# Down-projection of a transformer block: the subtraction for a chunk's own columns moved behind its block sums on VectorE

## The chip, the cores and the metric

The kernel runs on one core of a Trainium2 chip. The metric is the time of one execution on the device in microseconds (us), as the median of several executions. The profile is of one further execution, taken by the hardware profiler. Engines: TensorE (PE in the profile, PEld for its weight loads), VectorE (DVE), ScalarE (ACT), GpSimd (POOL) and SyncE (SP, here a DMA queue).

## The reference

One residual block on 512 tokens of width 1024: two attention branches with gates, then a gated convolutional feed-forward part, whose end is what this case is about.

```python
def conv_glu(x, w_up, conv_w, conv_b, w_down):
    hid = x @ w_up
    hid = lax.conv_general_dilated(hid, conv_w[:, None, :], window_strides=(1,),
        padding=((CONV_WIDTH - 1, 0),), dimension_numbers=('NWC', 'WIO', 'NWC'),
        feature_group_count=2 * D_FF) + conv_b
    gate, up = hid[..., :D_FF], hid[..., D_FF:]
    return (jax.nn.silu(gate) * up) @ w_down
...
    x = x + (sigmoid(g_A) * y_A + sigmoid(g_B) * y_B) @ w_out
    x = x + conv_glu(rms_norm(x, norm2_g), w_ffn_up, ffn_conv_w, ffn_conv_b, w_ffn_down)
```

The down-projection multiplies 512 x 2816 by 2816 x 1024, all in float32.

## The kernel before, in words

**Numbers in two parts.** A float32 matrix product is made of three matmuls of a reduced format (float32r): each operand is split into a high part (a cast, on ScalarE) and a low part (the original minus the cast, on VectorE), and high by high, high by low and low by high are added up in PSUM. For weights, the function `split_gen` issues the cast (line 148) and the subtraction (line 150).

**Chunks and loads.** The weights come in chunks of 1 MB or, for the down-projection, 0.5 MB, in a fixed order that `CHUNKS` lists. While TensorE multiplies with one chunk, `run_chunk` steps the generator that splits the next one, and when a chunk's split ends, the load of a later chunk goes to SyncE's queue (line 104). In the down-projection the raw weights lie in three thirds of a ring, each 1024 columns wide, and a chunk's load goes to the third of the chunk three before it. It waits until that chunk's readers are done.

**Fast matrix product.** The down-projection runs in two passes (`s` = 0, 1), each for 512 of the 1024 output columns, and each in 11 chunks of 256 of the 2816 inner columns. A chunk is a 2 x 2 product of blocks and is made in Winograd's form with 7 products (line 855 gives their order: 1, 2, 3, 6, 5, 7, 4) instead of 8. Each product has two tiles of 128 tokens and three matmuls of 256 columns each (lines 875 to 877), so a chunk has 42 matmuls. Of the weight operands, three of the seven are blocks of the raw chunk itself (its own columns, 768 wide; products 1, 2 and 3 use them), and four are sums and differences of blocks (1024 wide; products 6, 5, 7 and 4). `down_sums` makes these four on VectorE with three instructions (lines 118, 119 and 120), in a scratch area of 1024 columns that all chunks share. So a chunk is split in two pieces, with one cast and one subtraction each: first the own columns, then the sums.

**Where the split weights lie.** Up to the fifth chunk of the second pass the high and the low parts each have two buffers (`whi`, `wlo`), so that a cast waits for the end of the chunk before last. From the sixth chunk of the second pass they lie in a pool of eight (`hl`), whose buffers the operands `a` of the first eight chunks leave behind as they are used up.

**The order of instructions.** It is not that of the code: a planner simulates the engines and sorts the instructions of each engine by its own estimate of when they can run. `behind(ins, others)` (line 537) sets an order by hand, without a wait on the chip: the planner puts `ins` after `others` on their engine. `late["halves"]` is the last subtraction of a down-projection chunk, and each subtraction is put behind the one before it (line 153); some of the adds that put results together are put behind it too (lines 903, 905, 924, 927, 941). `late["casts"]` does the same for the casts.

**Putting together.** `fin0` and `rest0` combine the seven products of the first pass with adds (line 881 is the helper `add`), and `rest0` spreads its eight adds over the second pass's chunks, one for each, the last two at the very end. Each pass has seven product banks out of eight in PSUM, so that the second pass's products take over banks that the first pass's adds and copies free. In the second pass the last two chunks are multiplied together (`ends`, lines 991 to 1005): products 1, 6 and 2 of the one, then of the other, then product 5 of both, 7 of both, 4 of both, and at last 3. `fin1` adds them to the residual and stores: line 958 subtracts product 4, line 963 adds product 3 in two halves, and each result goes to a store.

Of the kernel before, what the change touches and what calls it, by code (L numbers as in the profile page):

```python
# [11 lines left out]
ALU = mybir.AluOpType  # L12
# [52 lines left out]
def block_kernel(ctx: ExitStack, tc: tile.TileContext, x, xt, params, g2, rbx, wts, wdn, out):  # L65
    nc = tc.nc
    V, A, G, PE, SP = nc.vector, nc.scalar, nc.gpsimd, nc.tensor, nc.sync
# [26 lines left out]
    raws, splits, late, ring = {}, {}, {}, []  # L94
# [18 lines left out]
    def down_sums(raw):  # L113

        b = raw.rearrange("p (b c) -> p b c", c=256)
        ts = ring[1][:, 1024:2048]
        t = ts.rearrange("p (b c) -> p b c", c=256)
        V.tensor_tensor(t[:, 0:2], b[:, 0:4:2], b[:, 0:2][:, ::-1], op=ALU.subtract)
        V.tensor_tensor(t[:, 2], b[:, 2], t[:, 0], op=ALU.subtract)
        V.tensor_tensor(t[:, 3], t[:, 2], b[:, 3], op=ALU.subtract)  # L120
        return ts

    def split_gen(i, pieces):
# [11 lines left out]
        if i >= FIRST_DN:  # L135

            if i < FIRST_DN + NP + 5:
                hi, lo = hi[:, 0:1792], lo[:, 0:1792]
            else:
                hl = late["pool"].tile([P, 3584], F32R, tag="ap", name=f"hl_{key}", bufs=8)  # L140
                hi, lo = hl[:, 0:1792], hl[:, 1792:3584]
            cuts, kn = [(0, raw[:, 256:1024]), (768, down_sums(raw))], 7
# [394 lines left out]
    def behind(ins, others):  # L537

        for o in others:
            tc.add_manual_dep(ins.ins, o.ins.name, mybir.DependencyInfo(  # L540
                mybir.DependencyClass.NoSync, mybir.DependencyReason.DATA), reason="table order")
        return ins
# [104 lines left out]
    for s in range(len(steps)):  # L647
# [6 lines left out]
        br, h, t, e = pend.pop(0)  # L654
# [171 lines left out]
    halves = []  # L826
# [51 lines left out]
        return prev  # L878

    def add(o, a, b, op=ALU.add, after=()):  # L880
        behind(V.tensor_tensor(o, a, b, op=op), after)

    def blk(x, r, c):

        return x[:, 2 * r:2 * r + 2, 256 * c:256 * (c + 1)]

    v3 = lambda ap: ap.rearrange("p (t c) -> p t c", t=2)
# [8 lines left out]
    def fin0(p):  # L896
        ps = banks[0][p]
        c = tmp["c"]
        if p == 1:
            tmp["u"] = fp.tile([P, S], F32, tag="cg", name="u_0", bufs=1)  # L900
            A.copy(tmp["u"], ps)
        elif p == 2:
            add(blk(c, 0, 0), v3(ps), v3(tmp["u"]), after=late["halves"])
        elif p == 6:
            add(tmp["u"], ps, tmp["u"], after=late["halves"])
        elif p == 5:
            tmp["v"] = fp.tile([P, 768], F32, tag="st", name="v_0", bufs=1)[:, 0:S]
            add(tmp["v"], ps, tmp["u"])
        elif p == 7:
            behind(A.copy(blk(c, 1, 1), v3(ps)), late["casts"])  # L910
        elif p == 4:
            behind(A.mul(blk(c, 1, 0), v3(ps), -1.0), late["casts"])
        else:
            behind(A.copy(blk(c, 0, 1), v3(ps)), late["casts"])
# [16 lines left out]
    def fin1(p):  # L931
        ps = banks[1][p]
        x = tmp["x"]

        def put(r, c):
            for t in range(2 * r, 2 * r + 2):
                SP.dma_start(out[0, t * P:(t + 1) * P, 512 + 256 * c:768 + 256 * c], x[:, t, 256 * c:256 * (c + 1)])
        if p == 1:
            tmp["u"] = fp.tile([P, S], F32, tag="cg", name="u_1", bufs=1)
            behind(A.copy(tmp["u"], ps), late["casts"])  # L940
            add(blk(x, 0, 0), v3(ps), blk(x, 0, 0), after=late["halves"])
        elif p == 6:
            add(tmp["u"], ps, tmp["u"])
        elif p == 2:
            add(blk(x, 0, 0), v3(ps), blk(x, 0, 0))
            put(0, 0)
        elif p == 5:
            tmp["v"] = fp.tile([P, 768], F32, tag="st", name="v_1", bufs=1)[:, 0:S]
            add(tmp["v"], ps, tmp["u"])
            add(blk(x, 1, 1), blk(x, 1, 1), v3(tmp["v"]))  # L950
            add(blk(x, 0, 1), blk(x, 0, 1), v3(tmp["v"]))
            add(blk(x, 1, 0), blk(x, 1, 0), v3(tmp["u"]))
        elif p == 7:
            add(blk(x, 1, 1), v3(ps), blk(x, 1, 1))
            put(1, 1)
            add(blk(x, 1, 0), v3(ps), blk(x, 1, 0))
        elif p == 4:
            add(blk(x, 1, 0), blk(x, 1, 0), v3(ps), op=ALU.subtract)
            put(1, 0)
        else:  # L960
            for t in range(2):
                o = x[:, t, 256:512]
                add(o, ps[:, 256 * t:256 * (t + 1)], o)
                (SP, A)[t].dma_start(out[0, t * P:(t + 1) * P, 768:1024], o)

    rest = iter(())
# [26 lines left out]
    for ps in ((1, 6, 2), (5,), (7,), (4,)):  # L993
        for i, (hi, lo) in ends:
            for p in ps:
                prev = product(1, p, i, hi, lo, prev=prev)
                if i == NP - 1:
                    fin1(p)
                    if p < 3:
                        for _ in range(2):  # L1000
                            next(rest, None)
    for t in range(2):
        for i, (hi, lo) in ends:
            prev = product(1, 3, i, hi, lo, (t,), prev)
    fin1(3)


# [39 lines left out]
```

## Time and profile before

| what | us |
|---|---|
| median of 3 runs | 749.35 (749.09 to 749.73) |
| the profiled execution, its own time | 749.92 |
| its span, first to last instruction | 748.2 |
| down-projection, first to last matmul | 626.0 to 744.1 |
| last matmul's end to the span's end | 4.05 |

How to read the profile: times are us from the start of the span, unless marked ns. A row of a timeline gives start, duration, engine, line of the kernel, operation, what it writes and reads, its shape, and how many instructions are merged in it; in brackets stands the idle time of the engine before it, and whose work ended it. A row of stretches gives the limits of the stretch, its length, the busy time of an engine with the number of instructions, the granted clock of TensorE as a share of full speed, the share of time in which the DMA engines were busy, and GB/s. The chain of waits follows the work that ended last backwards; a row gives start, length and what ran. Ends of matmuls are modelled: a busy TensorE need not be at its peak.

### The profile page before, as it was taken

What the parts mean: (1) busy time and instruction counts of PE and PEld (TensorE: products, weight loads), DVE (VectorE), ACT (ScalarE), POOL (GpSimd) and SP (SyncE); (2) the same over time, 40 slices, a digit from 0 to 9 for tenths busy, and PEclk for the clock granted to TensorE, in tenths of its full rate; (3) what the DMA queues carried; (4) which work ended last, traced back from release to release, by engine and by line L of the source; (5) the groups of instructions that cost most, each with busy time, mean ns of one, the idle gap of its engine ahead of it and who ended that gap; (6) DMA issues with size and microseconds to landing.
All of it is one profiled execution on the core that took longest, in us unless ns stands there. A gap on an engine that the chain in (4) does not pass through costs nothing.

```text
span 748.2 us, 10982 instructions
## 1 busy us (share of the span) xinstructions
PE 737.1 (99%) x4301; PEld 648.2 (87%) x4301; DVE 536.8 (72%) x984; ACT 377.3 (50%) x674; POOL 41.8 (6%) x73
## 2 busy tenths in 40 slices
PE   8999999999999999999999999999999999999996
PEld 7999998888988888888899888888888889999995
DVE  6588876776978886573476777676668767877776
ACT  6675565557856775432254544534444443434331
POOL 2701100001011011000000000000000000000000
PEclk9999999999999999999999999999999999999998
DMA  8632232122221131225341232233133211333442
GB/s 283 262 123 85 83 115 72 62 92 73 65 105 57 57 108 62 92 106 224 113 169 64 107 112 87 84 112 113 57 113 113 71 71 57 113 112 116 140 141 85
DMA packets 19205, 79.98 MB, mean 107 GB/s; under 512 B 2128, under 2 KB 4304, under 8 KB 13008
## 3 DMA queue, kind: packets, MB, share of 16 engines
q1 hardware_dynamic: 18864, 79.04, 30.2%
q8 instruction: 34, 0.56, 0.3%
q10 hardware_dynamic: 288, 0.23, 0.1%
q14 instruction: 19, 0.16, 0.1%
HBM read 75.07 MB, written 4.19 MB: 106 GB/s over the span
## 4 chain that ended last, share of the span: by engine, by line
PE 90%; DVE 5%; ACT 2%; issue 2%; DMA 1%; SPq 0%; DVEq 0%
PE pg L176 5%; PE pu L176 5%; PE pu L175 5%; PE pg L175 5%; PE pu L177 5%; PE pg L177 5%; PE P L876 3%; PE P L877 3%; PE P L875 3%; PE gA L175 2%; PE wo L176 2%; PE wo L177 2%; PE wo L175 2%; PE gA L177 2%; PE qkB L175 2%; PE gB L175 2%
## 5 line engine op out<-in xcount | busy, mean ns | idle before, releaser
L150 DVE TENSOR_TENSOR wlo_up<-raw_up,whi_up 128x1024 fp32r<-128x1024 f32 (+1 forms) x50 | 52.4, 1094 | 51.0 <-ACT whi_up L148 51.0
L176 PE MATMUL pu<-htl,whi_up 128*128 128x512 f32 (+1 forms) x192 | 72.1, 375 | 0.0
L176 PE MATMUL pg<-htl,whi_up 128*128 128x512 f32 (+1 forms) x192 | 72.0, 375 | 0.0
L175 PE MATMUL pu<-hth,whi_up 128*128 128x512 f32 (+1 forms) x192 | 71.7, 374 | 0.0
L175 PE MATMUL pg<-hth,whi_up 128*128 128x512 f32 (+1 forms) x192 | 71.7, 374 | 0.0
L177 PE MATMUL pg<-hth,wlo_up 128*128 128x512 f32 (+1 forms) x192 | 71.1, 370 | 0.0
L177 PE MATMUL pu<-hth,wlo_up 128*128 128x512 f32 (+1 forms) x192 | 71.0, 370 | 0.0
L148 ACT CAST whi_up<-raw_up 128x1024 fp32r<-128x1024 f32 (+1 forms) x50 | 44.6, 945 | 30.9 <-PE pu L176 27.2
L876 PE MATMUL P<-wlo_dn,a 128*128 128x256 f32 x224 | 59.2, 281 | 0.0
L877 PE MATMUL P<-whi_dn,a 128*128 128x256 f32 x224 | 59.0, 280 | 0.0
L875 PE MATMUL P<-whi_dn,a 128*128 128x256 f32 x224 | 50.3, 282 | 0.5 <-ACT whi_dn L148 0.5
L148 ACT CAST whi_dn<-raw_dn 128x768 fp32r<-128x768 f32 (+1 forms) x32 | 29.1, 942 | 42.8 <-DVE raw_dn L120 38.2
L150 DVE TENSOR_TENSOR wlo_dn<-raw_dn,whi_dn 128x768 fp32r<-128x768 f32 (+1 forms) x32 | 34.2, 1089 | 20.6 <-ACT whi_dn L148 20.5
L876 PEld LDWEIGHTS P<-wlo_dn,a 128*128 128x128 f32 x224 | 42.3, 189 | 0.3
L877 PEld LDWEIGHTS P<-whi_dn,a 128*128 128x128 f32 x224 | 42.3, 189 | 0.0
L175 PEld LDWEIGHTS pu<-hth,whi_up 128*128 128x128 f32 x192 | 36.0, 188 | 7.1
L175 PEld LDWEIGHTS pg<-hth,whi_up 128*128 128x128 f32 x192 | 36.0, 188 | 7.0
L177 PEld LDWEIGHTS pu<-hth,wlo_up 128*128 128x128 f32 x192 | 36.0, 188 | 6.7
L177 PEld LDWEIGHTS pg<-hth,wlo_up 128*128 128x128 f32 x192 | 36.0, 188 | 6.7
L176 PEld LDWEIGHTS pu<-htl,whi_up 128*128 128x128 f32 x192 | 36.1, 188 | 6.0
L176 PEld LDWEIGHTS pg<-htl,whi_up 128*128 128x128 f32 x192 | 36.1, 188 | 5.9
L875 PEld LDWEIGHTS P<-whi_dn,a 128*128 128x128 f32 x224 | 36.6, 188 | 1.2 <-ACT whi_dn L148 1.2
(260 smaller groups left out, 2065.7 us busy)
## 6 DMA issues: line engine op xcount, KB each, us to landing
raw_up<-in_wts SPq DMA_DIRECT2D x22, 1024.0 KB, 4.7
raw_dn<-in_wdn SPq DMA_DIRECT2D x22, 512.0 KB, 3.2
raw_gA<-in_wts SPq DMA_DIRECT2D x4, 1024.0 KB, 4.7
raw_qkB<-in_wts SPq DMA_DIRECT2D x4, 1024.0 KB, 4.7
raw_gB<-in_wts SPq DMA_DIRECT2D x4, 1024.0 KB, 4.7
raw_wo<-in_wts SPq DMA_DIRECT2D x4, 1024.0 KB, 4.7
xs<-in_xt SPq DMA_DIRECT2D x8, 256.0 KB, 5.0
xtok<-in_x SPq DMA_DIRECT2D x4, 512.0 KB, 7.7
```

What stands on the lines that cost most here:

```text
L148: cast = A.copy(hi[:, sl], src)
L150: ins = E.tensor_tensor(lo[:, sl], src, hi[:, sl].bitcast(F32), op=ALU.subtract)
L175: PE.matmul(ps, sh, mh, start=first, stop=False)
L176: PE.matmul(ps, sh, ml, start=False, stop=False)
L177: PE.matmul(ps, sl, mh, start=False, stop=last)
L875: behind(PE.matmul(dst, sh, mh, start=first and t == 0, stop=False, skip_group_check=True), prev)
L876: PE.matmul(dst, sh, ml, start=False, stop=False, skip_group_check=True)
L877: prev = (PE.matmul(dst, sl, mh, start=False, stop=last, skip_group_check=True),)
```

## The change

In `down_sums`, the last of the three instructions is added to `late["halves"]`. The first subtraction of the same chunk's split, that of the own columns, is issued right after, and so is put behind it: on VectorE the order within a chunk becomes sums, own columns' subtraction, sums' subtraction. Before, nothing set the order between the sums and the own columns' subtraction. From the own columns' subtraction on, `late["halves"]` is what it was.

The second part is at the end of the second pass: the subtraction of product 4 (line 958) is kept in `late["p4"]`, and the two adds of product 3 (line 963), the product issued last, are put behind it on VectorE.

```diff
@@ -117,7 +117,9 @@
         t = ts.rearrange("p (b c) -> p b c", c=256)
         V.tensor_tensor(t[:, 0:2], b[:, 0:4:2], b[:, 0:2][:, ::-1], op=ALU.subtract)
         V.tensor_tensor(t[:, 2], b[:, 2], t[:, 0], op=ALU.subtract)
-        V.tensor_tensor(t[:, 3], t[:, 2], b[:, 3], op=ALU.subtract)
+        ins = V.tensor_tensor(t[:, 3], t[:, 2], b[:, 3], op=ALU.subtract)
+
+        late["halves"] = late.get("halves", ()) + (ins,)
         return ts
@@ -878,7 +880,7 @@
     def add(o, a, b, op=ALU.add, after=()):
-        behind(V.tensor_tensor(o, a, b, op=op), after)
+        return behind(V.tensor_tensor(o, a, b, op=op), after)
@@ -955,12 +957,12 @@
         elif p == 4:
-            add(blk(x, 1, 0), blk(x, 1, 0), v3(ps), op=ALU.subtract)
+            late["p4"] = (add(blk(x, 1, 0), blk(x, 1, 0), v3(ps), op=ALU.subtract),)
             put(1, 0)
         else:
             for t in range(2):
                 o = x[:, t, 256:512]
-                add(o, ps[:, 256 * t:256 * (t + 1)], o)
+                add(o, ps[:, 256 * t:256 * (t + 1)], o, after=late["p4"])
                 (SP, A)[t].dma_start(out[0, t * P:(t + 1) * P, 768:1024], o)
```

## The prediction

> **What bounds the kernel now.** I read the page first, then TensorE's matmuls of the down-projection by stretches of time, then the rounds of VectorE and ScalarE that feed them. The page says that TensorE is the bound:
>
> ```profile
> span 748.2 us, 10982 instructions
> PE 737.1 (99%) x4301; PEld 648.2 (87%) x4301; DVE 536.8 (72%) x984; ACT 377.3 (50%) x674; POOL 41.8 (6%) x73
> ```
>
> That is an average. The change touches only the down-projection, 22 chunks of 42 matmuls (7 products, 2 token tiles, 3 matmuls each). The next rows are busy time and, in brackets, the number of matmuls on the product banks P in each stretch; behind it the granted clock. The two rows below them are from the chain of waits, where TensorE is the chain.
>
> ```profile
> 642.00:696.00 54.00, 54.00 (x463) 1.00 0.39 127
> 696.00:728.20 32.20, 32.05 (x254) 1.00 0.40 132
> 728.20:735.90 7.70, 4.55 (x31) 1.00 0.00 0
> 735.90:739.30 3.40, 3.40 (x18) 0.50 0.41 154
> 739.30:744.20 4.90, 4.85 (x40) 1.00 0.32 107
> 696.00:744.20 48.20, 44.85 (x338) 0.96 0.33 110
> ```
> ```profile
> 649.00 0.82 PE P L875 x7
> 653.95 0.82 PE P L875 x7
> ```
>
> Two rows of the chain, one chunk apart, give the undisturbed pitch: 4.95 us for 42 matmuls, 117.9 ns each. At that pitch the 338 matmuls from 696.0 to 744.2 need 39.85 us; they took 48.2. So **8.35 us are lost in the last eight chunks**, though the busy column calls TensorE busy for 44.85 of them (a matmul's span there is 0.28 us, so busy time hides a gap of 0.1 us). In the same way 254 x 0.1179 = 29.95 of 32.2 (2.25 lost), 3.65 of 7.7 (4.05 lost), 2.1 of 3.4 (1.3 lost, at half the clock), 4.7 of 4.9. (A matmul over an edge counts in both stretches, so these parts come out a little under the whole.)
>
> Who makes TensorE late? One round of VectorE, and ScalarE's rows beside it:
>
> ```profile
> 703.26 1.23 DVE L150 TENSOR_TENSOR wlo_dn<-raw_dn,whi_dn 128x1024 fp32r<-128x1024 f32 x1 [1.12 <-ACT whi_dn L148]
> 704.41 0.68 DVE L881 TENSOR_TENSOR c<-c,v 128x512 f32<-128x512 f32 x1
> 705.01 0.95 DVE L150 TENSOR_TENSOR hl_dn<-raw_dn,hl_dn 128x768 fp32r<-128x768 f32 x1
> 705.88 0.68 DVE L118 TENSOR_TENSOR raw_dn<-raw_dn 128x512 f32<-128x512 f32 x1
> 706.60 0.42 DVE L119 TENSOR_TENSOR raw_dn<-raw_dn,raw_dn 128x256 f32<-128x256 f32 x1
> 707.05 0.43 DVE L120 TENSOR_TENSOR raw_dn<-raw_dn,raw_dn 128x256 f32<-128x256 f32 x1
> 708.59 1.23 DVE L150 TENSOR_TENSOR hl_dn<-raw_dn,hl_dn 128x1024 fp32r<-128x1024 f32 x1 [1.11 <-ACT hl_dn L148]
> ```
> ```profile
> 707.51 1.79 ACT L148 CAST hl_dn<-raw_dn 128x1024 fp32r<-128x1024 f32 x2 [3.55 <-DVE raw_dn L120]
> ...
> 732.97 1.04 ACT L148 CAST hl_dn<-raw_dn 128x1024 fp32r<-128x1024 f32 x1 [2.94 <-DVE raw_dn L120]
> ```
>
> I call the 768-wide subtraction of L150 (own columns) lo0 and the 1024-wide one (block sums) lo1, and ScalarE's casts before them hi0 and hi1. The round is a closed chain: lo1 (1.15 to the next start), an add of the first pass (0.60), lo0 (0.87), the sums of L118 to L120 (705.88 to 707.48, 1.60), hi1 with its two handovers (707.48 to 708.59, 1.11), and lo1 again: 5.33 us, against TensorE's 4.95. VectorE idles 1.11 of it for hi1, and ScalarE 3.55 for the sums. hi0 of that round was cast long before. Each round with an add puts VectorE 0.38 further behind; when the head start is used up, TensorE waits, in about six chunks for some 0.4 us each. In the last two chunks the products 1, 6 and 2 of both come first, so that lo1 of the last chunk is wanted sooner, and it gets dear:
>
> ```profile
> 729.34 0.38 PE L875 MATMUL P<-hl_dn,a 128*128 128x256 f32 x1 [0.22 <-ACT hl_dn L148]
> 730.60 0.39 PE L876 MATMUL P<-hl_dn,a 128*128 128x256 f32 x1 [0.88 <-DVE hl_dn L150]
> 734.06 0.38 PE L875 MATMUL P<-hl_dn,a 128*128 128x256 f32 x1 [1.18 <-ACT hl_dn L148]
> 735.32 0.39 PE L876 MATMUL P<-hl_dn,a 128*128 128x256 f32 x1 [0.88 <-DVE hl_dn L150]
> ```
>
> Right behind these four gaps the granted clock is 0.50 for 3.4 us (the row from 735.90 above), the only such stretch under matmuls of this stage.
>
> **Part 1: lo0 behind the sums.** No instruction is added or removed; lo0 only trades places with L118 to L120. The sums write one scratch area that lo1 of the chunk before reads, so they still start behind that lo1, and hi1 follows them. But lo0 now runs while hi1 is cast: 0.87 to 0.95 under a wait of 1.11. The round becomes 1.15 + 0.60 + 1.60 + 1.11 = 4.46 us with an add, 3.86 without, both under 4.95: TensorE becomes the bound to the end. One cost does not show: L118 right behind the lo1 whose input it overwrites. From the rows, L119 behind the L118 whose result it reads starts 0.72 after it (0.04 past its end), while L118 behind an unrelated lo0 starts 0.08 before that ends. So the bound is 0 to 0.12 a round, and it cannot be negative, as both instructions stay. I take 0.05; even 4.58 is under 4.95.
>
> The last chunks ask for a lead. 18 matmuls (2.1 us) after its start a chunk needs lo1. Where two buffers hold the split weights, hi0 waits for the end of the chunk before last, that is until the chunk ahead of its own starts; lo1 is then done after 0.83 + 1.05 + 1.23 = 3.1 us, and is needed after 4.95 + 2.1 = 7.1: a lead of 4. From the sixth chunk of the second pass the weights have a pool of eight, that wait goes, and the shorter rounds add 0.4 to 0.5 for each of about three with an add, 1.0 for each of three without. The last chunk's lo1 is wanted 24 matmuls after the last but one starts (2.8 instead of 7.1), 4.2 us sooner. A lead of some 8 covers that, so all four gaps go, and with them, I hold, the half clock: gain 8.35.
>
> **What it costs at the start of the stage.** lo0 waits behind the sums in every chunk, and TensorE's first product waits for lo0. Where the head start is small this shows. The first chunk whose order changes:
>
> ```profile
> 638.99 0.95 DVE L150 TENSOR_TENSOR wlo_dn<-raw_dn,whi_dn 128x768 fp32r<-128x768 f32 x1
> 639.87 0.68 DVE L118 TENSOR_TENSOR raw_dn<-raw_dn 128x512 f32<-128x512 f32 x1
> ...
> 641.79 0.42 DVE L120 TENSOR_TENSOR raw_dn<-raw_dn,raw_dn 128x256 f32<-128x256 f32 x1
> ```
> ```profile
> 641.93 0.28 PE L876 MATMUL P<-wlo_dn,a 128*128 128x256 f32 x1
> ```
>
> The sums move up by lo0's 0.87, to end at 641.34; lo0 ends at 642.3; TensorE wants it at 641.93. Loss 0.3 to 0.4, once; if an activation copy that lies between L118 and L119 there slips, none or 0.6. I take 0.3. In later chunks lo0 is done 1.8 us (0.83 + 0.95) into the chunk before, 3.1 ahead of need.
>
> **Loads, and part 2.** The load of the chunk three ahead goes into the columns that the sums, hi0 and lo0 read; its last reader is now lo0, not L120:
>
> ```profile
> SPq L104 <- DVE raw_dn L120: 64.3, 15, 5.2
> ```
> ```profile
> DMA to landing us min/median/max: 3.1/3.3/3.3
> ```
>
> The release comes 0.95 behind L120, in a round that is 0.87 shorter, and the data are wanted three rounds later (over 11 us) against 3.3 of landing: hidden, with 7 us of cover. What is behind it on SyncE's queue, the stores of the first pass's result, shifts by under 1 us with nobody waiting. Part 2 puts the adds of product 3, issued last, behind the subtraction of product 4; that is their order already, and they wait for TensorE's last matmul:
>
> ```profile
> 743.20 0.69 DVE L881 TENSOR_TENSOR x<-x,P 128x512 f32<-128x512 f32 x1
> 744.19 0.75 DVE L881 TENSOR_TENSOR x<-P,x 128x256 f32<-128x256 f32 x2 [0.30 <-PE P L877]
> ```
>
> Its price is 0: it keeps an order. So the 4.05 us from there to the span's end stay.
>
> **Sum.** 8.35 - 0.3 = 8.05 off. The profiled execution took 749.92 (748.2 of span); its span would be 740.15. The median of the runs shown, 749.35, is 0.57 below that execution; from it, 749.35 - 8.05 = **741.3 us**.
>
> **The rivals.** *The half clock stays* (0.08): 1.3 us of the gain are the stretch at 0.50. The longest idle ahead of it is 1.18, four gaps in 6 us; if the fall comes of something else, such as the end of the work, it stays, and the time is 742.6. The Trainium skill, page "TensorE: Matmul & The Clock Gate", section "Why this matters for your kernels", asks only that no gap between bursts be over some 3 us, and by it these gaps would not halve the clock; the row of 0.50 right behind them speaks against that.
>
> *The pass boundary gets a new stall* (0.09). A planner sorts the instructions. Around 683 the adds that free product banks of the first pass for the second stand in VectorE's queue:
>
> ```profile
> 683.20 0.69 DVE u L881
> 684.05 0.35 issue
> 684.40 0.68 DVE v L881
> ```
>
> If it puts the next lo0 ahead of them, they wait for that chunk's hi0, and so for TensorE; TensorE's next products wait for the banks: some 1.5 to 2 us, once: 743.1. Against it: VectorE is then earlier than now.
>
> *Nothing moves* (0.05): TensorE is the bound, and no work is taken from it. 99% speaks for it, the count at the pitch against it. 749.4. The Trainium skill, page "Perfetto Trace Analysis", section "Identifying the Most-Contended Engine", says to optimize the engine of the highest occupancy first, which would be TensorE; it also warns that matmul busy time misleads, and by its other measure, weight loading, the page's 87% leaves room.
>
> *Slower* (0.03): lo0 and hi1 hinder each other when they run side by side. If lo1 then starts only 0.95 + 1.11 behind the sums, the round is 1.15 + 0.60 + 1.60 + 2.06 = 5.41, no shorter than before, and lo0 comes 1.6 later for the first product: 0.08 to 0.15 a chunk more over eight chunks and the 0.3 at the start, with the gaps left: 750.5. It decides once the overlap costs over 0.9 a round. Against it: the second cast of the row at 707.51 begins at about 708.5 and overlaps lo1 at 708.59, and both have their usual length.
>
> **How the numbers follow.** The forecast has 0.75. The bounds of the adjacent L118 and of the start give 740.9 to 741.7, the spread of the runs half a microsecond more; half clock and boundary reach 742.6 and 743.1, both with the start's 0.6 to 744. So 740.3 to 744.0, which leaves out little but the last two rivals. About 0.2% (1.5 us) is what a measurement can tell from none: faster 0.92, same 0.05, slower 0.03.
>
> **What would show it.** In the changed kernel's rounds the 1024-wide L150 should wait for ScalarE under 0.3 us instead of 1.11, with the 768-wide one between L120 and it. From 696 on, matmuls should come at 4.95 a chunk, no row of TensorE in the last chunks should wait on the split weights, and the granted clock should be 1.00 until the matmuls end, near 736. A new gap of 0.3 should stand near 642. The last matmul to the end should stay at 4 us. It is wrong if VectorE's round stays over 4.95, if gaps remain at the last two chunks, or if new waits on banks show near 682.

## The result, and the profile after

The changed kernel takes 740.38 us (median of 4 runs, 739.67 to 742.14) against 749.53 before (749.09 to 749.73): a ratio of 0.9882, with a 95% interval from 0.9864 to 0.9901. That is 9.15 us faster, just inside the low end of the range and 0.9 below the forecast. The forecast knew only a part of this: the gaps that it meant were worth 7.9 us, and 2.0 more came, in the execution that was profiled, from something that it does not know.

The head of the page of the changed kernel and its chain of waits by engine; the last row is the chain of the kernel before. In the profiles of changed kernels the lines behind `down_sums` are two or more higher than before (here L152 is the L150 of before, L883 the L881).

```profile
span 737.9 us, 10983 instructions
PE 730.8 (99%) x4301; PEld 644.2 (87%) x4301; DVE 538.0 (73%) x984; ACT 378.1 (51%) x674; POOL 42.1 (6%) x73
...
PE 96%; DMA 2%; ACT 0%; SPq 0%; DVE 0%; issue 0%; POOL 0%; DVEq 0%
```
```profile
PE 90%; DVE 5%; ACT 2%; issue 2%; DMA 1%; SPq 0%; DVEq 0%
```

TensorE's share is 99% and its weight loads have 87%, exactly as before: neither figure shows a change that took 10.3 us off the span. The chain does: TensorE now makes 96% of it, and VectorE, which had 5%, is gone.

Matmuls of the down-projection by stretches (busy time, number of matmuls, granted clock, as before):

```profile
642.00:696.00 54.00, 54.00 (x478) 1.00 0.41 137
696.00:728.20 32.20, 32.20 (x275) 1.00 0.38 132
728.20:733.90 5.70, 5.66 (x48) 1.00 0.24 80
```

From 696.0 to 728.2 stand 275 matmuls where 254 stood, the stretch with the four gaps has no gap left, and the clock is 1.00 to the end of the matmuls at 733.86. One round of VectorE in the same place of the program, and ScalarE's casts beside it:

```profile
704.96 1.23 DVE L152 TENSOR_TENSOR hl_dn<-raw_dn,hl_dn 128x1024 fp32r<-128x1024 f32 x1 [0.25 <-ACT hl_dn L150]
706.10 0.68 DVE L883 TENSOR_TENSOR c<-c,x 128x512 f32<-128x512 f32 x1
706.71 0.68 DVE L118 TENSOR_TENSOR raw_dn<-raw_dn 128x512 f32<-128x512 f32 x1
707.42 0.43 DVE L119 TENSOR_TENSOR raw_dn<-raw_dn,raw_dn 128x256 f32<-128x256 f32 x1
707.89 0.42 DVE L120 TENSOR_TENSOR raw_dn<-raw_dn,raw_dn 128x256 f32<-128x256 f32 x1
708.23 0.95 DVE L152 TENSOR_TENSOR hl_dn<-raw_dn,hl_dn 128x768 fp32r<-128x768 f32 x1
709.43 1.23 DVE L152 TENSOR_TENSOR hl_dn<-raw_dn,hl_dn 128x1024 fp32r<-128x1024 f32 x1 [0.25 <-ACT hl_dn L150]
```
```profile
708.34 1.78 ACT L150 CAST hl_dn<-raw_dn 128x1024 fp32r<-128x1024 f32 x2 [2.68 <-DVE raw_dn L120]
```

The own columns' subtraction (lo0, at 708.23) runs while the sums are cast (from 708.34), and VectorE waits 0.25 for that cast instead of 1.11. The round is 709.43 - 704.96 = 4.47 us; it was 5.33.

To see where the time went, I take from both traces the start of each chunk's first matmul (42 matmuls a chunk, in order) and subtract the chunk's durations. Chunks are counted from 1 to 22, 12 to 22 being the second pass.

| chunks | saved, us | what it is |
|---|---|---|
| ahead of the stage | 0.44 | from one execution to another: two executions of one program, further down, differ by 1.96 here |
| 1 to 3 | 0.00 | same gaps in both |
| 4 | -0.08 | the new wait for lo0 |
| 5 to 13 | 1.64 | no gaps in either; the matmuls follow each other faster |
| 14 | 0.00 | |
| 15, 16 | 1.11 | 0.74 gaps, 0.37 faster matmuls |
| 17 to 20 | 1.51 | gaps |
| 21, 22 | 5.67 | the four gaps and the half clock |
| last matmul to the end | -0.03 | |
| sum | 10.26 | span 748.20 to 737.93 |

So the gaps and the half clock are worth 0.74 + 1.51 + 5.67 = 7.92 us, the faster matmuls 2.01.

### The profile page after: what moved, and what is told of

It is laid out like the page before. It is cut to its first block, busy times and chain, and to the rows that moved or that the text cites. A ratio compares the mean times of both kernels' runs of the same rounds, so it can differ in the third digit from the quotient of the medians.

```text
span 737.9 us, 10983 instructions
## 1 busy us (share of the span) xinstructions
PE 730.8 (99%) x4301; PEld 644.2 (87%) x4301; DVE 538.0 (73%) x984; ACT 378.1 (51%) x674; POOL 42.1 (6%) x73
## 4 chain that ended last, share of the span: by engine, by line
PE 96%; DMA 2%; ACT 0%; SPq 0%; DVE 0%; issue 0%; POOL 0%; DVEq 0%
PE pg L178 6%; PE pu L178 6%; PE pu L177 5%; PE pg L177 5%; PE pu L179 5%; PE pg L179 5%; PE P L878 5%; PE P L879 5%; PE P L877 5%; PE gA L177 2%; PE wo L178 2%; PE wo L177 2%; PE wo L179 2%; PE gA L179 2%; PE qkB L179 2%; PE gB L177 2%
## 5 line engine op out<-in xcount | busy, mean ns | idle before, releaser
L152 DVE TENSOR_TENSOR wlo_up<-raw_up,whi_up 128x1024 fp32r<-128x1024 f32 (+1 forms) x50 | 52.4, 1093 | 51.0 <-ACT whi_up L150 51.0
L879 PE MATMUL P<-whi_dn,a 128*128 128x256 f32 x224 | 60.4, 277 | 0.0
L150 ACT CAST whi_up<-raw_up 128x1024 fp32r<-128x1024 f32 (+1 forms) x50 | 44.5, 944 | 30.9 <-PE pu L178 27.2
L877 PE MATMUL P<-whi_dn,a 128*128 128x256 f32 x224 | 57.6, 278 | 0.5 <-ACT whi_dn L150 0.5
L150 ACT CAST whi_dn<-raw_dn 128x768 fp32r<-128x768 f32 (+1 forms) x32 | 29.2, 943 | 34.4 <-issue 14.9
L152 DVE TENSOR_TENSOR wlo_dn<-raw_dn,whi_dn 128x768 fp32r<-128x768 f32 (+1 forms) x32 | 34.8, 1091 | 12.2 <-ACT whi_dn L150 12.1
L879 PEld LDWEIGHTS P<-whi_dn,a 128*128 128x128 f32 x224 | 42.1, 188 | 0.0
L877 PEld LDWEIGHTS P<-whi_dn,a 128*128 128x128 f32 x224 | 40.0, 188 | 1.0 <-ACT whi_dn L150 1.0
```

Of the source, the lines that this page charges most:

```text
L150: cast = A.copy(hi[:, sl], src)
L152: ins = E.tensor_tensor(lo[:, sl], src, hi[:, sl].bitcast(F32), op=ALU.subtract)
L877: behind(PE.matmul(dst, sh, mh, start=first and t == 0, stop=False, skip_group_check=True), prev)
L879: prev = (PE.matmul(dst, sl, mh, start=False, stop=last, skip_group_check=True),)
```

## The experiments

The theory: VectorE and ScalarE go round a closed chain (sums' subtraction, sums of the next chunk, their cast, its subtraction), and lo0 stood in it; behind the sums it hides under the cast. The main rival was that TensorE's own pace makes the gain. Ratios are to the kernel before, run on the same chip.

**The first part alone.** The diff against the changed kernel:

```diff
-                add(o, ps[:, 256 * t:256 * (t + 1)], o, after=late["p4"])
+                add(o, ps[:, 256 * t:256 * (t + 1)], o)
```

> Only the first part: the own columns' subtraction behind the block sums; the order of the last two adds is left to the planner, which in this kernel puts the two adds of product 3 ahead of product 4's subtraction on VectorE. Theory: the whole gain is in the first part, so 740 to 741.5 against 749.5 before; the tail from the last matmul to the end grows by about 0.7 us (one 128x512 subtraction of 0.69 us, and its stores, now behind the last matmul), from 4.3 to about 5. Rival: the second part carries a share of the gain, then over 742.

Measured: 743.28 us (741.31 to 744.75), ratio 0.9927 (0.9904 to 0.9950), slower than expected and in the rival's range. The stage is that of the changed kernel, chunk by chunk within 0.02 us, and the last matmul ends at 733.65. The span ends at 739.58, so the tail is 5.93 us instead of 4.07: 1.9 longer, where 0.7 was expected. VectorE's last rows of this kernel, and its stores on SyncE's queue:

```profile
733.69 0.76 DVE L883 TENSOR_TENSOR x<-P,x 128x256 f32<-128x256 f32 x2 [0.96 <-PE P L879]
734.36 0.68 DVE L883 TENSOR_TENSOR x<-x,P 128x512 f32<-128x512 f32 x1
```
```profile
734.14 0.33 SPq L966 DMA_DIRECT2D out<-x  x1
735.07 0.83 SPq L939 DMA_DIRECT2D out<-x  x2
```

The subtraction of product 4, which could have run a microsecond earlier, stands behind adds that wait for TensorE's last matmul, VectorE idles 0.96 us, and two more stores are issued at the very end, one behind the other. The second part carries 1.9 us of the result in the profile, but only beside the first part. The medians of the two kernels, from two comparisons, lie 2.9 apart (740.38 and 743.28); the trace explains 1.9 of that.

**The second part alone.** Against the kernel before, only the diff's last two edits.

> Only the second part: product 3's adds held behind product 4's subtraction, nothing else. Theory: that was their order already, so the time is that of the kernel before, 749.5 within 0.5, and the four gaps at the last two chunks and the half clock behind them are there. Rival (the second part carries a share of the gain): under 748.

Measured: 749.62 us, ratio 1.0008 (0.9999 to 1.0018): nothing, as expected. Gaps and half clock are there. It does nothing by itself, because the planner had that order already; the first part makes the planner turn it, and the second part turns it back.

**The first part in one pass only.** In `down_sums`, with the chunk's number `i`:

```diff
-        late["halves"] = late.get("halves", ()) + (ins,)
+        if i >= FIRST_DN + NP:
+            late["halves"] = late.get("halves", ()) + (ins,)
```

(for the second pass; `i < FIRST_DN + NP` for the first).

> Both parts, but the first only in the chunks of the second pass. Theory (closed round): all gaps of the second pass go, 7.9 us, as VectorE gains its lead there. What the changed kernel gained beside that, 2.0 us by a shorter pitch of the matmuls (113.4 instead of 117.9 ns in chunks 5 to 13 and 15 to 16), should be lost in the first pass if the pitch is a state that the last wait leaves behind (the small gap near 644.6 stays here): 117.9 from there on, 742 to 743. Rival (the pitch follows from the buffers that the weights lie in): 113.4 all the same, 740.5.

Measured: 741.92 us (740.82 to 742.84), ratio 0.9910 (0.9890 to 0.9930). Chunks 15 to 22 save 0.73 + 1.51 + 5.67 = 7.91 us, every gap, and chunks 5 to 16 run at 117.9 ns. So the gaps are worth what the theory says, by themselves, at a pitch that did not change, and all of them can be had from the second pass. By the medians of this comparison (748.81 before) the kernel saves 6.9 us; the interval of the ratio leaves room for 5.2 to 8.2.

> Both parts, but the first only in the chunks of the first pass. Theory (closed round): the second pass starts with the lead of the changed kernel, some 4 us, and loses 0.4 to 0.6 in each of six rounds with an add (5.33 us against 4.76 to 4.95), so that gaps come back late, at the last two chunks above all: 2 to 4 us of gaps, perhaps with a half clock behind them, 743 to 746. Rival (the gain is made in the first pass, by the pitch): under 742.

Measured: 743.05 us (741.60 to 744.05), ratio 0.9924 (0.9904 to 0.9944). The lead that the first pass leaves lasts to chunk 20; in chunk 21 it is used up, and TensorE waits once, 1.2 us from one matmul to the next:

```profile
728.70 0.33 PE L878 MATMUL P<-hl_dn,a 128*128 128x256 f32 x1
729.90 0.38 PE L879 MATMUL P<-hl_dn,a 128*128 128x256 f32 x1 [0.87 <-DVE hl_dn L153]
```

Expected were 2 to 4 us of gaps; it was 1.2. The clock stays 1.00 behind this one gap. The lead does what the prediction used it for: it is made in one place and spent in another.

**lo0 behind the sums' subtraction.** The sums still come first, but lo0 no longer lies under the cast:

```diff
-            ins = E.tensor_tensor(lo[:, sl], src, hi[:, sl].bitcast(F32), op=ALU.subtract)
...
+            for o2, src2 in [(o, src)] if i < FIRST_DN else cuts[::-1] if j else []:
+                sl = slice(o2, o2 + src2.shape[-1])
+                ins = E.tensor_tensor(lo[:, sl], src2, hi[:, sl].bitcast(F32), op=ALU.subtract)
+                if i >= FIRST_DN:
+                    late["halves"] = (behind(ins, late.get("halves", ())),)
```

> The changed kernel with one more turn: the own columns' subtraction comes behind the sums' subtraction, so that on VectorE the order is sums, sums' subtraction, own columns' subtraction. The sums still come first; only the overlap with the cast is gone. Theory (the gain is that overlap): the round is 5.33 us with an add again, VectorE waits 1.11 for the cast again, the gaps come back: 748.5 to 751. Rival (the gain is that the sums come first): 740 to 742.

Measured: 750.67 us (748.42 to 752.07), ratio 1.0010 (0.9995 to 1.0026). VectorE's round in this kernel:

```profile
713.85 2.09 DVE L156 TENSOR_TENSOR hl_dn<-raw_dn,hl_dn 128x1024 fp32r<-128x1024 f32 x2 [1.11 <-ACT hl_dn L150]
715.86 0.68 DVE L885 TENSOR_TENSOR c<-c,x 128x512 f32<-128x512 f32 x1
...
719.18 2.09 DVE L156 TENSOR_TENSOR hl_dn<-raw_dn,hl_dn 128x1024 fp32r<-128x1024 f32 x2 [1.11 <-ACT hl_dn L150]
```

719.18 - 713.85 = 5.33 us, the old round with the old wait of 1.11, and the last eight chunks take 47.8 us, as good as the 48.2 before: the gaps are back. The rival that the sums' place alone makes the gain falls; it is the overlap. That the whole time is the old one too is in part chance: chunks 3 and 4, where lo0 now comes later, take 2.5 us longer than before, and chunks 5 to 11 run at 113.4 ns and take 1.3 less.

**lo0 on GpSimd.** Against the kernel before:

```diff
-            E = G if i == 2 else V
+            E = G if i == 2 or (i >= FIRST_DN and j == 0) else V
...
-                late["halves"] = (behind(ins, late.get("halves", ())),)
+                late["halves"] = (behind(ins, late.get("halves", ())),) if j else late.get("halves", ())
```

> The kernel before with one edit: in the down-projection the subtraction of the own columns runs on GpSimd, not on VectorE; the order of the sums is left to the planner. Theory (closed round): without the 0.87 us of that subtraction the round is 1.15 + 0.60 + 1.60 + 1.11 = 4.46 us, as in the changed kernel, and TensorE's gaps go: 740 to 742.5, as long as GpSimd needs under 3 us for a 128x768 subtraction. If GpSimd needs more than 4.9, it is the new bound and the time is over 749. Rival (the order on VectorE is what counts, not the length of the round): 749.

Measured: 767.77 us, ratio 1.0250 (1.0233 to 1.0266). A miss, and GpSimd is not too slow: it needs 2.15 us. Its row, and VectorE's round beside it:

```profile
721.21 2.15 POOL L150 TENSOR_TENSOR hl_dn<-raw_dn,hl_dn 128x768 fp32r<-128x768 f32 x1 [3.96 <-ACT hl_dn L148]
```
```profile
720.43 1.23 DVE L150 TENSOR_TENSOR hl_dn<-raw_dn,hl_dn 128x1024 fp32r<-128x1024 f32 x1 [1.11 <-ACT hl_dn L148]
721.58 2.33 DVE L881 TENSOR_TENSOR c<-c,u 128x512 f32<-128x512 f32 x1
723.83 0.68 DVE L118 TENSOR_TENSOR raw_dn<-raw_dn 128x512 f32<-128x512 f32 x1
...
726.54 1.23 DVE L150 TENSOR_TENSOR hl_dn<-raw_dn,hl_dn 128x1024 fp32r<-128x1024 f32 x1 [1.11 <-ACT hl_dn L148]
```

The add that took 0.68 takes 2.33 and ends 0.55 behind GpSimd's subtraction, as if it had stood still while that ran. The Trainium skill, page "SBUF — State Buffer", section "Who interferes with whom", says that a VectorE instruction with two SBUF inputs contends with a GpSimd one that reads SBUF, and calls the ports that they share an exclusive lock; these rows agree. So lo0's work did not leave the chain, it came back as 2.25 us from the add to the sums. The round is 726.54 - 720.43 = 6.11 us = 1.15 + 2.25 + 1.60 + 1.11, and chunks 18 to 20 take 6.1 us each: TensorE follows the length of the round here too.

**The pitch of the matmuls**, the time from the start of one to the start of the next. The number of matmuls from 650 to 690 us, where none of the kernels has a gap, and from 704 to 720, in one fence for each kernel: the kernel before; the changed one; the one with the first part in the second pass only; in the first pass only; and that last one again.

```profile
650.00:690.00 40.00, 40.00 (x342) 1.00 0.33 104
704.00:720.00 16.00, 16.00 (x127) 1.00 0.35 116
```
```profile
650.00:690.00 40.00, 40.00 (x356) 1.00 0.40 135
704.00:720.00 16.00, 16.00 (x135) 1.00 0.48 166
```
```profile
650.00:690.00 40.00, 40.00 (x342) 1.00 0.32 110
```
```profile
650.00:690.00 40.00, 40.00 (x342) 1.00 0.38 124
```
```profile
650.00:690.00 40.00, 40.00 (x355) 1.00 0.38 121
```

342, or 355 to 356, and nothing between: from start to start 117.9 or 113.4 ns, at a granted clock of 1.00 both times. What fixes it?

> The changed kernel itself once more, for its time beside the next three and for the pitch of its matmuls in a second profiled execution. If the pitch is set by the waits before it and these come alike in each execution: 113.4 ns again in chunks 3 to 16, 740 to 740.5. If it is a matter of chance in each execution: 117.9 in some stretch, and a time up to 2.3 us longer (12 chunks x 0.19).

Measured: 740.83 us (739.93 to 742.17), ratio 0.9888 (0.9873 to 0.9904), and 113.4 ns in chunks 5 to 16 again.

> The same kernel as the one with the first part in the first pass only, looked at again for the pitch of its matmuls: 117.9 ns from chunk 4 to 16 in its first profiled execution, while five kernels with the same order of matmuls there and the same wait in chunk 4 had 113.4. If the pitch after a wait is a matter of chance in each execution, it may be 113.4 here, and the matmuls then end 2.2 us sooner; if it is fixed by the program, 117.9 again.

Measured (one execution): 744.05 us, and 113.4 ns, where the first execution of the very same program had 117.9. Ahead of its chunk 4 it is the other way round: 117.9 in chunk 3, where the first had 113.4. So the program alone does not fix it. Nor does the chip: the two executions were on different chips, but the first chip had shown 113.4 with the first part alone, and on the second one the next kernel shows 117.9. The stage is 2.0 us shorter here (109.8 against 111.8), and the execution as a whole is no faster, as its first matmul of the stage comes 1.96 later (627.35 against 625.39), from what lies ahead of the change.

> The same kernel as the one with the first part in the second pass only, looked at again for the pitch: 117.9 ns from chunk 5 to 16 in its first profiled execution. If chance decides after each wait, 113.4 may show here from some wait on, and the time falls by 0.19 us for each chunk of it; if the program fixes it, 117.9 from chunk 5 on again.

Measured (one execution): 742.78 us, 117.9 ns in chunks 5 to 16 again. In all these traces the pitch changes only in the few matmuls behind one that waited, or where the weights' buffers change; in one place, at 689 in the kernel before, the ones ahead of the change are only 3 to 8 ns late, and no row shows a wait. What decides which of the two it becomes stays open. 12 chunks at the one pitch or the other differ by 12 x 0.19 = 2.2 us; the runs of the changed kernel spread over 2.5, which would fit, but those of the kernel before spread over 2.2 to 3.0 in the later comparisons too (748.03 to 750.23, 748.03 to 750.25, 748.25 to 751.23), and executions that were not profiled don't show their pitch.

**The pool of eight buffers.** From chunk 17 on the changed kernel's matmuls come every 120.0 ns, and 704 to 720 lies there. Both kernels change the chunk from which the split weights lie in the pool (both places):

```diff
-        if i < FIRST_DN + NP + 5:
+        if i < FIRST_DN + NP + 11:
```

(none of them; `+ 9` leaves only the last two chunks there).

> The changed kernel with the split weights of all chunks in the two buffers of each kind, none in the pool of eight. Theory: the pitch of 120.0 ns in the last six chunks comes of the pool's buffers, so they come at 113.4 and 1.7 us are gained (6 x 42 x 6.6 ns); but the cast of the last chunk's own columns waits for the end of the chunk before last but one, so its sums' subtraction is done 3.2 us after the last but one starts and is wanted after 2.7: 0.5 of gaps. Net 1.0 to 1.5 faster than the changed kernel. Rival (the pitch comes of the time in the program or of what runs beside it): 120 stays and the gaps cost 0.5: slower by 0.5.

Measured: 740.58 us (739.51 to 742.65), ratio 0.9889 (0.9872 to 0.9905). The matmuls come at 113.4 ns to the end, 143 of them from 704 to 720; chunk 21 takes 0.64 us more than that pitch gives (5.40 against 4.76), most of it in one wait for the last subtraction, where 0.5 was expected, and the tail is 0.54 longer (4.61 against 4.07), which was not expected and whose cause is open. From the first to the last matmul the stage takes 107.2 us against 108.2: the gain of 1.0 is there, and half of it is given back in the tail; the times show no difference.

> The changed kernel with only the last two chunks' weights in the pool of eight. If the pool's buffers make the pitch of 120.0 ns: four chunks more at 113.4, 4 x 42 x 6.6 ns = 1.1 us faster than the changed kernel, with no gaps at the last two. Rival: 120 stays from the same time on, no difference.

Measured: 739.90 us (738.08 to 741.83), ratio 0.9872 (0.9853 to 0.9890), the lowest of all. Chunks 17 to 20 come at 113.4 ns, no gap, the stage takes 107.1 us, 1.1 less than in the changed kernel. The profile shows the gain; the times, whose intervals overlap, do not separate the two. From 704 to 720, first with no chunk in the pool, then with the last two:

```profile
704.00:720.00 16.00, 16.00 (x143) 1.00 0.29 100
```
```profile
704.00:720.00 16.00, 16.00 (x143) 1.00 0.50 166
```

So the 120.0 belongs to the pool's buffers and not to the time in the program. Whether it is their place, or that high and low part lie in one buffer, was not tried.

## Why the prediction was right, and where its numbers were off

**The closed round** was right, in mechanism and size. The prediction has 4.46 us with an add; it is 4.47. Without one it has 3.86 and it is 3.99: the sums right behind the lo1 whose input they overwrite start 1.26 behind it instead of 1.15, the upper bound that the prediction set and did not take; with an add between, nothing is lost. VectorE's wait for the cast is 0.25, under the 0.3 that it named.

**The gaps.** 8.35 was forecast, 7.92 measured. The term of the sum that was mis-sized is the one pitch of 117.9 ns for all eight chunks: from chunk 17 on the floor is 120.0, so that some 0.5 us of the "loss" were never to be had. Its sign, matmuls at 4.95 us a chunk from 696 on, did not show for the same reason: they came at 4.76 up to chunk 16 and at 5.04 behind it.

**The lead.** Some 8 was forecast against the 4.2 that the last chunks' order wants, so 3.8 to spare. The last lo1 ends at 723.10; it is wanted 24 matmuls of 120 ns after chunk 21 starts at 723.62, at 726.5: 3.4 to spare.

**The cost at the start.** The gap at the fourth chunk is there, 0.2 us instead of 0.3. lo0 ends at 641.78, and the matmul that wants it could have started at 641.72, one pitch behind the row above it; it and the next one each start 0.22 behind the one before, instead of 0.11:

```profile
641.61 0.28 PE L879 MATMUL P<-whi_dn,a 128*128 128x256 f32 x1
641.83 0.38 PE L878 MATMUL P<-wlo_dn,a 128*128 128x256 f32 x1
```

The prediction took the wrong row for the matmul that wants lo0: the one at 641.93 still belongs to the chunk before. In that trace the weight load that waits for VectorE is at 642.05 and its matmul at 642.16, so that lo0's end at 642.3 was 0.1 late and not 0.4.

**The half clock** went with the gaps, as held; the rival that it stays fell. In the four kernels whose trace has the cluster of gaps at the last two chunks (before, the second part alone, lo0 behind lo1, lo0 on GpSimd) the clock falls to 0.50 for 3.4 us right behind it; in the nine profiles with one such gap there, at most a small one beside it, or none, it falls only after the last matmul.

**The pass boundary** made no stall. The planner spread the adds that free the banks between the sums, 4 us earlier than before:

```profile
678.73 0.68 DVE L118 TENSOR_TENSOR raw_dn<-raw_dn 128x512 f32<-128x512 f32 x1
679.33 0.68 DVE L883 TENSOR_TENSOR u<-P,u 128x512 f32<-128x512 f32 x1
679.93 0.41 DVE L119 TENSOR_TENSOR raw_dn<-raw_dn,raw_dn 128x256 f32<-128x256 f32 x1
680.26 0.68 DVE L883 TENSOR_TENSOR v<-P,u 128x512 f32<-128x512 f32 x1
```

**"Part 2 ... its price is 0: it keeps an order"** was right for the two orders compared, and incomplete as a reading of the edit. The prediction took the order of the trace before as given, though it says elsewhere that a planner sorts the instructions; the first part gives the planner another timeline, and without the second the tail is 1.9 us longer.

**What it did not see** is the pitch: 2.0 us of the profiled 10.3. That the median still lies in the range, 0.08 above its low end, is luck. "TensorE becomes the bound to the end" was right, but the bound itself was taken as fixed at 4.95 us a chunk. Without the 2.0, the sum 749.53 - 7.92 + 0.08 is 741.7, next to the forecast; the kernel with the first part in the second pass only, whose pitch stayed at 117.9, is that case, and took 741.92.

## What to carry to other kernels

When two engines hand work to each other and one of them idles for the other's step in every round, write the round out as a closed chain; work that is not part of the chain belongs under the wait, and a reordering is then worth its full duration in each round, until another engine's pace is reached. Judge a busy engine by counting its instructions against the pitch of an undisturbed stretch: busy shares of 99% and 99% stood on both sides of this change. And where a planner sorts the queues, an edit at one place can turn an order at another, so the tail has to be looked at again, and an order that matters has to be pinned.

## What the runs showed of the hardware

The same matmuls (128 x 128 by 128 x 256, float32r, each with its own weight load) ran at three pitches at a full granted clock: 113.4, 117.9 and 120.0 ns. The first two change places behind a wait (once, in the kernel before, behind starts that are 3 to 8 ns late) and then last for hundreds of matmuls (12 chunks of 42 here), and one program showed both in two executions; the third goes with the buffers that the split weights lie in.

And gaps far shorter than the stretch of half clock behind them go with it: those before the change were 0.22, 0.88, 1.18 and 0.88 us within 6 us. The Trainium skill, page "TensorE: Matmul & The Clock Gate", section "Why this matters for your kernels", asks to avoid idle gaps over some 3 us; here a cluster of shorter ones stood ahead of it each time, so the measurement decides. The longest single gap does not tell the traces apart: one of 1.73 us, with lo0 on GpSimd, ahead of the matmul at 689.99, has no half clock behind it, and neither has the one of 0.87 in the kernel with the first part in the first pass only. The number of matmuls in a step of time does. The records of the clock in these traces last multiples of 3.413 us where they end within the profile (3.41, 6.83 and 10.24; 730.45 is 214 of them). In steps of that length, counted from the start of the half clock, the step right ahead of it has 6 or 7 starts of matmuls in the four kernels that have it under matmuls (6 from 732.49 to 735.90 in the kernel before, where 28 would fit at 120 ns). No other step of the stage, in any of the thirteen traces, has fewer than 13, and behind all of these the clock is 1.00. No run was made to try this, or the cluster, as the cause by itself.
